# Hybrid block on one core: VectorE's splits ordered two by two behind its reads of banks in the Down stage, the forget column copied by VectorE, filler between attention's first score pieces

## The chip, the cores and the metric

The kernel runs on one core of one Trainium2 chip. The metric is the device time of one execution in microseconds. The core has five engines that work from queues of their own: TensorE (PE in the profile) multiplies matrices and writes the results into the eight banks of PSUM, VectorE (DVE) and ScalarE (ACT) read those banks and work elementwise, GpSimd (POOL) works elementwise on SBUF alone, and SyncE (SP) issues most of the DMAs. Each engine takes its instructions strictly in the order of its queue.

## The reference

One layer of a streaming encoder, on 16 meta tokens followed by 1,024 tokens of 1,024 features, all in float32:

```
h   = concat(meta, x)
xn  = rmsnorm(h)
q, k, v, f, u, gates = split(xn @ w_in)
F   = cumsum(log_sigmoid(f + b_forget))            # one column per head, 8 heads
p   = softmax(q k^T / 8 + F[t] - F[s], s <= t)
y_a = (p v) @ w_attn_out
z   = gelu(s5(u)) @ w_glu;   y_s = z_left * sigmoid(z_right)
h   = h + (sigmoid(g1) * y_a + sigmoid(g2) * y_s) @ w_o
xn  = rmsnorm(h)
a   = conv3(xn @ w_up);      h = h + (silu(a_gate) * a_val) @ w_down      # 2,816 hidden features
out = rmsnorm(h) without the meta tokens
```

## The kernel before, in words

**Precision.** A float32 operand is used as two parts of a shorter format. ScalarE copies it into the short format (the high part); the low part is the operand less its high part, a subtraction called a *split* (`split_lo`, L136, whose instruction carries line L137). Each product is then three matmuls: high by high, high by low, low by high. A split by VectorE or GpSimd has two inputs in SBUF, unless its source lies in a bank.

**Order.** A planner places each engine's instructions by a simulation of the whole program; a call `after(a, b)` (L132) adds that a stands behind b in its engine's queue, without a wait. In attention TensorE's order is written out by hand (`pin`).

**The stages**, with their places in the span: projections of u and the state-space part with the gates (to about 180 us); the projection of q and k for the first pair of heads, the forget rows and the gated product of z (to about 310 us); the values; attention (343 to 620 us); the output products (to 745 us); the feed-forward products (to 1220 us); and the Down stage (to the end).

**The forget rows** (`forget_steps`, L551). They run as a side line while `project_qk(0)` (L593) projects k. VectorE takes the absolute value, ScalarE exponential and logarithm (L555), VectorE a minimum (L558) and the cumulative sum by a scan (L559). The columns are held in two halves, one on partitions 0 to 7, the other on 32 to 39. ScalarE copies the last column of the first half, 8x1, into `ct` (L560); VectorE's L561 adds it to the second half and scales; GpSimd's queue stores both halves to `f_d` (L563). Around it ScalarE copies k out of the banks (L608, L611), and VectorE takes its low parts.

**The gated product** (`glu`, L684) follows, by `seven` (L215): a 2x2 block product in seven block products instead of eight. `weight_forms` (L258) makes seven operands out of four weight blocks: sums on GpSimd (`sf`, L699), high parts on ScalarE (`ops`, L693), low parts on VectorE or, for two of seven, on GpSimd. In `seven` the first product's bank is copied by ScalarE into `c` (L243) before the third product may go on adding into that bank; the second product's bank is added to `c` by VectorE (L240).

**Attention.** Units of work are a pair of heads, a group of two or three row tiles and a head of the pair. For each row tile `scores` (L826) issues two matmuls into a bank of the two called `sp` (L853, L854); VectorE reads it with the forget row added and a running minimum (L859), ScalarE exponentiates (L864), GpSimd scales (L866). `scores` yields after each bank. Between such pieces TensorE gets *filler*, matmuls of the next pair's projections and of the gates, by `take(n)` (L954), which takes n of them from a stream. Before the loop over units stands a lead (L1037 to L1043): 24 filler matmuls, the first tiles' scores of unit 0, 7 filler, its last tile's scores, 14 filler, the first scores of unit 1, 7 filler. What is left of pair 0's filler is spread over its units.

**The Down stage** (from L1481). The product with `w_down` is again seven block products, numbered 0 to 6, for each of four groups of two or three pairs of row blocks: `groups = [(8, 9), (7, 0, 1), (2, 3, 4), (5, 6, 10)]`, taken in the order 0, 4, 1, 2, 5, 3, 6. A product (`product`, L1628) has four tiles of 128 rows, each in a bank of its own: two sets of four banks (`mm`, `mm`, `mm`, `po` and `sp`, `tp`, `sp`, `tp`) take turns. Products 4, 5 and 6 go on adding into the banks of 0, 1 and 3 (`JOINS`), once these have been read. VectorE reads each tile's bank and adds it into the result (L1657); the instructions that do so are appended to `first_add`. Three tiles of operands make 9 matmuls per bank and 36 per product.

`forms(p, j)` (L1517) makes the operands of product p for pair j: a load of the weight sum, for most pairs an in-place sum of the activations on GpSimd (L1526 for product 1, L1528 for 2, L1530 for 3, L1532 for 6), two high parts on ScalarE (L1539) and two splits, by GpSimd for products 0, 4 and 5 and by VectorE for 1, 2, 3 and 6 (L137). `prepare` (L1689), called ahead of each `product`, issues the forms as far ahead as the 14 operand slots allow: in the middle groups, three products. The next group's activations are loaded into tiles that the last in-place use of this group sets free. Some orders are there already: splits of group 0 and the last splits of the last group are put behind certain reads by `after`.

Of the kernel before, what the change touches and what calls it, by code (L numbers as in the profile page):

```python
# [25 lines left out]
H = 8  # L26
# [32 lines left out]
def block_kernel(ctx, tc, x, meta, xbt, x0t, g1t, w_q, w_k, w_v, w_f, w_u, w_g, b_f, w_ao, lam_d, bw_d, cw_d,  # L59
# [5 lines left out]
    V, S, GP, PE, SY = nc.vector, nc.scalar, nc.gpsimd, nc.tensor, nc.sync  # L65
# [66 lines left out]
    def after(inst, first):  # L132
        tc.add_manual_dep(inst.ins, first.ins.name, mybir.DependencyInfo(
            mybir.DependencyClass.NoSync, mybir.DependencyReason.DATA), reason="order")

    def split_lo(eng, out_, src, hi):  # L136
        return eng.tensor_tensor(out_, src, hi.bitcast(F), ALU.subtract)  # L137
# [74 lines left out]
    def m_ps():  # L212
        return pp.tile([P, 512], F, tag="mm", name="mm", bufs=3)
# [193 lines left out]
    for k0, n in FIRST:  # L407
        j, sl = k0 // 2, slice(k0 % 2, k0 % 2 + n)
# [120 lines left out]
    HL = L // 2  # L529
# [21 lines left out]
    def forget_steps(fl_, fx, ct, behind):  # L551
        after(V.scalar_tensor_tensor(out=fx, in0=fl_, scalar=-1.0, in1=fl_, op0=ALU.mult, op1=ALU.max), behind)
        for k_ in (dict(func=AF.Exp, scale=-1.0), dict(func=AF.Ln, bias=one[:FR])):
            ev = yield
            act = S.activation(fx, fx, **k_)  # L555
            after(act, ev)
            yield act
        V.scalar_tensor_tensor(out=fx, in0=fl_, scalar=0.0, in1=fx, op0=ALU.min, op1=ALU.subtract)  # L558
        V.tensor_tensor_scan(fl_, one[:FR].broadcast_to([FR, HL]), fx, 0.0, ALU.mult, ALU.add)  # L559
        S.copy(ct[32:], fl_[:H, HL - 1:])  # L560
        V.tensor_scalar(fx, fl_, ct, -8.0, ALU.add, ALU.mult)  # L561
        for r, a in ((0, 0), (32, HL)):
            GP.dma_start(f_d[:, a:a + HL], fx[r:r + H])  # L563
        yield
# [255 lines left out]
    def pin(inst):  # L820
        if pinned[0] is not None:
            after(inst, pinned[0])
        pinned[0] = inst
        return inst
# [129 lines left out]
    def take(n):  # L954
        for _ in range(n):
            mm = next(stream, None)
            if mm is not None:
                pin(mm)
# [30 lines left out]
    def fill_of(pr):  # L989
        gens, cnt = [], 0  # L990
        if pr < last_pair:
            tiles_of[pr + 1] = qk_tiles(pr + 1)
            gens.append(project_qk(pr + 1, tiles_of[pr + 1]))
            cnt += QKN
        for i in range(sum(GA[:pr]), sum(GA[:pr + 1])):
            gens.append(gate_chunk(i, ap, True))
            cnt += GAN
        return chain_(*gens), cnt
# [24 lines left out]
    def scores_of(u, which):  # L1023
        if u >= len(units):
            return
        pr, cs, e = units[u]
        if which == 0 and cs[0] == 0:
            if e == 0 and pr == last_pair:
                spares.append(spare_tiles())
            fb = ap.tile([P, L], F, tag="fb", name="fb", bufs=2)  # L1030
            SY.dma_start(fb, f_d[2 * pr + e].partition_broadcast(P))
            fbs[pr, e] = fb
        done = pts_of.setdefault(u, [])
        for c in tiles_at(u, which):
            yield from scores(tiles_of[pr], e, c, fbs[pr, e], done)

    stream, cnt = fill_of(0)  # L1037
    take(24)
    cnt -= 24
    for u, which, n in ((0, 0, 7), (0, 1, 14), (1, 0, 7)):  # L1040
        for _ in scores_of(u, which):
            pass
        take(n)  # L1043
        cnt -= n
    for u, (pr, cs, e) in enumerate(units):
        if cs[0] == 0 and e == 0:
            if pr:
                stream, cnt = fill_of(pr)
# [432 lines left out]
    groups = [(8, 9), (7, 0, 1), (2, 3, 4), (5, 6, 10)]  # L1481
# [35 lines left out]
    def forms(p, j):  # L1517
        b_ = down1.tile([P, 512], F, tag="w", name="wr", bufs=8)
        behind(SY.dma_start(b_, w_block(*own_w[p], j) if p in own_w else t_d[p][P * j:P * j + P]), j)

        if j not in SUMMED:
            r = pairs[j]
            a11, a21, a12, a22 = (r[k, h_] for k in range(2) for h_ in range(2))
            sub, add = ALU.subtract, ALU.add
            if p == 1:
                GP.tensor_tensor(a11, a11, a21, sub)  # L1526
            elif p == 2:
                GP.tensor_tensor(a11, a22, a11, add)  # L1528
            elif p == 3:
                GP.tensor_tensor(a21, a22, a21, sub)  # L1530
            elif p == 6:
                GP.tensor_tensor(a11, a11, a12, sub)  # L1532
            a_ = (a11, a11, a11, a21, a12, a22, a11)[p]
        else:
            a_ = load_form(p, j)
        slot = ops.pop(0)
        eng = GP if p in (0, 4, 5) else V
        for q, src in ((0, a_), (2, b_)):
            hi = S.copy(slot[q], src)  # L1539
            if first_copy and j in groups[0] and p >= 5:  # L1540
                after(hi, first_copy[1])
            cut = split_lo(eng, slot[q + 1], src, slot[q])
            if first_add and eng is V and j in groups[0] and p > 2:
                after(cut, first_add[1 if p == 3 else 3])
            if eng is V and j in groups[-1] and p == 6:
                after(cut, first_add[-1])
        return slot

    first_add, first_copy = [], []

# [75 lines left out]
    def product(g, p, slots, first, last):  # L1628
        l_, r_ = HALF
        joins = p in JOINS  # L1630
        whole = (0, 512)
        parts = [(t, whole) for t in range(4)]
        if last and p in (3, 6):
            parts[3:] = [(3, (0, 288)), (3, (288, 224))]
            if p == 3:
                held["end"] = m_ps()
        bks = banks(g, p)
        for t, (c0, n) in parts:
            bk = held["end"] if last and p in (3, 6) and c0 else bks[t]
            top, bot = hs[t], hs[4 + t]  # L1640
            to_, o = {0: (u2[t], 0), 1: (bot, 512), 2: (u2[t], 0), 3: (bot, 512),
                      4: (top, 0), 5: (bot, 0), 6: (top, 512)}[p]
            ts_ = slice(P * t, P * t + P)
            ps = bk[:, c0:c0 + n]
            for i, (ah, al, bh, bl) in enumerate(slots):
                k_ = dict(skip_group_check=True)
                PE.matmul(ps, ah[:, ts_], bh[:, c0:c0 + n], start=(i == 0 and not joins), stop=False, **k_)  # L1647
                PE.matmul(ps, ah[:, ts_], bl[:, c0:c0 + n], start=False, stop=False, **k_)  # L1648
                PE.matmul(ps, al[:, ts_], bh[:, c0:c0 + n], start=False, stop=(i == len(slots) - 1), **k_)  # L1649
            to = to_[:, o + c0:o + c0 + n]  # L1650
            if first and p == 0:
                first_copy.append(S.copy(to, ps))
            elif first and p in (1, 5):

                S.activation(to, ps, AF.Copy, scale=-1.0 if p in MINUS else 1.0)
            else:
                first_add.append(V.tensor_tensor(to, to, ps, ALU.subtract if p in MINUS else ALU.add))  # L1657
            if g == 2 and p == 3:
                GP.dma_start(bot, h_d[P * (4 + t):P * (4 + t) + P], accum_op=ALU.add)
            if last and p == 6:  # L1660
                row_done(t, slice(512 + c0, 512 + c0 + n), first_add[-1], t == 3)
                if t == 3 and c0:
                    rows_end(t)
                continue
            if last and n == 288:
                continue
            if not last:
                continue
            if p in (2, 1, 5):
                d_, op = {2: (bot[:, l_], ALU.add), 1: (bot[:, r_], ALU.subtract), 5: (top[:, r_], ALU.subtract)}[p]  # L1670
                GP.tensor_tensor(d_, d_, u2[t], op)
            if p in (5, 3):
                after(add_square(*sums_.pop(0)), first_add[-1])
            if p == 4:
                sums_.append((t, square(t, l_)[0]))
            elif p == 5:
                sums_.append((4 + t, square(4 + t, l_)[0]))
                GP.tensor_tensor(top[:, l_], top[:, l_], gfB[:, l_], ALU.mult)
                GP.tensor_tensor(bot[:, l_], bot[:, l_], gfB[:, l_], ALU.mult)
            elif p == 3:  # L1680
                row_done(4 + t, r_, first_add[-1])
# [37 lines left out]
    for g, p in turns:  # L1719
        prepare()  # L1720
        if (g, p) == (1, 0):
            SY.dma_start(gfB, gf.partition_broadcast(P))
        product(g, p, ready[g, p], g == 0, g == len(groups) - 1)
        ops += ready[g, p]


# [402 lines left out]
```

## Time and profile before

| | |
|---|---|
| median of 3 runs | 1434.75 us (1433.96 to 1434.91) |
| the profiled execution | 1433.68 us, its span 1431.9 us |
| TensorE clock granted | 0.998 |
| DMA | 216.17 MB, 151 GB/s in the mean |

In the rows of the trace, an instruction is given with its start and duration, engine, line, operation, the tile that it writes and those it reads, its shape, and in brackets the time that its engine stood idle before it and what ended that. Matmuls of one queue overlap: the next starts before the one before has ended. The stages by the busy time of the engines, a row per stretch:

```profile
155.00:330.00 175.00, 173.31 (x1200) 164.60 (x1199) 125.28 (x214) 86.83 (x177) 87.05 (x113) 1.00 0.49 134
330.00:620.00 290.00, 287.73 (x1992) 277.37 (x1991) 179.25 (x631) 152.41 (x358) 148.66 (x287) 1.00 0.35 95
...
1220.00:1432.00 212.00, 201.70 (x902) 166.62 (x900) 165.08 (x208) 93.05 (x183) 166.61 (x122) 0.99 0.53 167
```

The columns are the stretch, its length, then the busy time and number of instructions of TensorE, of its weight loads, of VectorE, ScalarE and GpSimd, the granted clock, the busy share of the DMA engines and GB/s.

### The profile page before, as it was taken

To read this page: it belongs to the slowest core of one execution; us is meant where nothing else is said; L and a number is where in the kernel's file an instruction comes from. 1 tells how busy PE (TensorE), PEld (TensorE's weight loads), DVE (VectorE), ACT (ScalarE), POOL (GpSimd) and SP (SyncE) were. 2 spreads that over 40 slices of the span, in tenths; PEclk is the share of its full clock that TensorE was granted. 3 is DMA by queue.
4 is the path that set the end of the run, shared out by engine and by line. 5 is a ranking of instruction groups with operands and counts; after the bars stand their busy time and mean duration, and the time that the engine had idled before them with its cause. 6 is when DMAs were issued, how large, how long until landed. Compare 5 with 4: busy or idle time off the path is not lost.

```text
span 1431.9 us, 26324 instructions
## 1 busy us (share of the span) xinstructions
PE 1411.9 (99%) x9607; PEld 1335.8 (93%) x9607; DVE 1069.9 (75%) x2050; ACT 710.2 (50%) x1382; POOL 757.1 (53%) x869
## 2 busy tenths in 40 slices
PE   8999999999999999999999999999999999999997
PEld 8999999988999999999889999999999999887886
DVE  7999788843667675666479977778876776788867
ACT  7647575423555555534546444444444345643433
POOL 1542248642456547326771344645546544887795
PEclk9999999999999999999999999999999999999999
DMA  8685645530156532077953246666753327964343
GB/s 307 169 184 160 161 98 152 157 119 30 53 155 163 124 95 72 23 267 270 225 156 130 74 111 184 182 183 166 177 141 121 97 79 250 332 204 144 109 94 118
DMA packets 93318, 216.17 MB, mean 151 GB/s; under 512 B 14802, under 2 KB 22610, under 8 KB 92804
## 3 DMA queue, kind: packets, MB, share of 16 engines
q1 hardware_dynamic: 74340, 170.28, 36.4%
q0 software_dynamic: 17696, 41.29, 15.1%
q10 hardware_dynamic: 1152, 2.91, 0.6%
q8 instruction: 76, 1.25, 0.4%
q14 instruction: 54, 0.44, 0.1%
HBM read 170.88 MB, written 71.71 MB: 169 GB/s over the span
## 4 chain that ended last, share of the span: by engine, by line
PE 56%; issue 1%; DVE 0%; POOLq 0%; DVEq 0%; ACT 0%; POOL 0%; ACTq 0%
PE sp L235 4%; PE sp L234 4%; PE sp L236 4%; PE tp L235 2%; PE tp L234 2%; PE tp L236 2%; PE mm L236 2%; PE mm L234 2%; PE mm L235 2%; PE mm L1649 2%; PE mm L1648 2%; PE mm L1647 2%; PE mm L1314 2%; PE mm L1315 2%; PE mm L1313 2%; PE sp L1647 1%
## 5 line engine op out<-in xcount | busy, mean ns | idle before, releaser
L172 PE MATMUL mm<-xhi,whi 128*128 128x342 f32 (+2 forms) x480 | 156.0, 325 | 0.0
L173 PE MATMUL mm<-xlo,whi 128*128 128x342 f32 (+2 forms) x480 | 155.4, 324 | 0.0
L174 PE MATMUL mm<-xhi,wlo 128*128 128x342 f32 (+2 forms) x480 | 154.4, 322 | 0.0
L1269 POOL TENSOR_TENSOR ov<-ov,og 128x1024 f32<-128x1024 f32 x21 | 50.8, 2420 | 119.6 <-ACT og L1268 117.2
L137 DVE TENSOR_TENSOR sw<-sf,sw 128x512 fp32r<-128x512 f32 x72 | 71.7, 996 | 45.2 <-ACT sw L1260 44.2
L1260 ACT CAST sw<-sf 128x512 fp32r<-128x512 f32 x72 | 44.9, 623 | 110.5 <-POOL sf L1407 79.4
L172 PEld LDWEIGHTS mm<-xhi,whi 128*128 128x128 f32 x480 | 90.4, 188 | 1.1 <-issue 0.6
L174 PEld LDWEIGHTS mm<-xhi,wlo 128*128 128x128 f32 x480 | 90.3, 188 | 0.5
L173 PEld LDWEIGHTS mm<-xlo,whi 128*128 128x128 f32 x480 | 90.4, 188 | 0.4
L1407 POOL TENSOR_TENSOR sf<-raw,sf 128x512 f32<-128x512 f32 x36 | 62.4, 1732 | 38.8 <-DVE sw L137 38.7
L236 PE MATMUL mm<-xhi,sw 128*128 128x258 f32 (+1 forms) x288 | 81.0, 281 | 0.0
L234 PE MATMUL mm<-xhi,sw 128*128 128x258 f32 (+1 forms) x288 | 80.8, 280 | 0.0
L1407 POOL TENSOR_TENSOR sf<-raw 128x512 f32<-128x512 f32 x36 | 48.7, 1352 | 60.6 <-DVE sw L137 32.1
L235 PE MATMUL mm<-xlo,sw 128*128 128x258 f32 (+1 forms) x288 | 80.7, 280 | 0.0
L864 ACT ACTIVATE pt<-pt,mx 128x400 f32<-128x400 f32 (+5 forms) x72 | 53.1, 737 | 45.7 <-DVE mx L859 45.3
L866 POOL TENSOR_SCALAR pt<-pt,mx 128x400 f32<-128x400 f32 (+5 forms) x72 | 51.8, 720 | 33.2 <-DVE mx L865 26.3
L1459 DVE SCALAR_TENSOR_TENSOR ov<-hv,cwt,ov 128x1024 f32<-128x1024 f32 x36 | 68.1, 1892 | 0.4 <-ACT ov L1457 0.4
L1260 ACT CAST sw<-raw 128x512 fp32r<-128x512 f32 x70 | 43.1, 622 | 47.4 <-PE sp L236 25.0
L904 ACT CAST th<-tp 128x512 fp32r<-128x512 f32 (+1 forms) x80 | 43.4, 542 | 37.3 <-PE tp L901 27.9
L137 DVE TENSOR_TENSOR sw<-raw,sw 128x512 fp32r<-128x512 f32 x70 | 57.9, 831 | 4.1 <-ACT sw L1260 3.9
L137 DVE TENSOR_TENSOR tl<-tp,th 128x512 fp32r<-128x512 f32 (+1 forms) x80 | 50.7, 634 | 10.7 <-ACT th L904 10.1
L835 POOL CAST qz<-q 64x128 fp32r<-64x128 f32 (+1 forms) x72 | 20.2, 283 | 69.4 <-PE sp L854 68.1
(722 smaller groups left out, 5724.5 us busy)
## 6 DMA issues: line engine op xcount, KB each, us to landing
raw<-in_w_up_dram SPq DMA_DIRECT2D x44, 512.0 KB, 3.7
t_d<-in_w_dn_dram POOLq DMA_DIRECT2D x44, 256.0 KB, 6.8
wr<-t_d SPq DMA_DIRECT2D x44, 256.0 KB, 3.3
ar<-a_d SPq DMA_DIRECT2D x41, 256.0 KB, 4.8
a_d<-ov SPq DMA_DIRECT2D x18, 512.0 KB, 2.6
wr<-in_w_dn_dram SPq DMA_DIRECT2D x33, 256.0 KB, 3.7
t_d<-in_w_dn_dram SPq DMA_DIRECT2D x22, 256.0 KB, 4.3
t_d<-t_d SPq DMA_DIRECT2D x22, 256.0 KB, 5.4
```

The source lines that it names most:

```text
L137: return eng.tensor_tensor(out_, src, hi.bitcast(F), ALU.subtract)
L172: yield PE.matmul(ps, whi[:, i, :], ahi[:, i], start=(i == 0), stop=False)
L173: yield PE.matmul(ps, whi[:, i, :], alo[:, i], start=False, stop=False)
L174: yield PE.matmul(ps, wlo[:, i, :], ahi[:, i], start=False, stop=(i == k - 1))
L234: PE.matmul(ps, a[0][:, i], bh, start=(i == 0 and not joins), stop=False, skip_group_check=True)
L235: PE.matmul(ps, a[0][:, i], bl, start=False, stop=False, skip_group_check=True)
L236: PE.matmul(ps, a[1][:, i], bh, start=False, stop=(i == kh - 1), skip_group_check=True)
L864: S.activation(pt[:n, :kc], pt[:n, :kc], AF.Exp, bias=low, scale=-1.0, accum_out=nm[:n, 0:1])
L866: GP.tensor_scalar(pt[:n, :kc], pt[:n, :kc], nm[:n, 1:2], 1.0, ALU.mult, ALU.mult)
L1260: S.copy(hi, src)
L1407: sums.append(GP.tensor_tensor(f_, a, b, op))
L1459: V.scalar_tensor_tensor(out=o, in0=h_[:, j:SEQ + j], scalar=cwc(j, m), in1=o, op0=ALU.mult, op1=ALU.add)
```

## The change

Three edits. In the Down stage, VectorE's splits for groups 1 and 2 that were issued since the last product are collected; once the next product is issued, splits 0 and 1 are put behind its first read of a bank in VectorE's queue, 2 and 3 behind the second, and so on. The forget column is copied by VectorE instead of ScalarE. In the lead of attention the filler is taken after each score piece instead of after all of them: 4 + 4, 14, 4 + 4 matmuls instead of 7, 14, 7.

```
@@ forget_steps
         V.tensor_tensor_scan(fl_, one[:FR].broadcast_to([FR, HL]), fx, 0.0, ALU.mult, ALU.add)
-        S.copy(ct[32:], fl_[:H, HL - 1:])
+        V.tensor_copy(ct[32:], fl_[:H, HL - 1:])
@@ the lead of attention
-    for u, which, n in ((0, 0, 7), (0, 1, 14), (1, 0, 7)):
+    for u, which, n in ((0, 0, 4), (0, 1, 14), (1, 0, 4)):
         for _ in scores_of(u, which):
-            pass
-        take(n)
-        cnt -= n
+            take(n)
+            cnt -= n
@@ forms
             cut = split_lo(eng, slot[q + 1], src, slot[q])
+            if eng is V and j in (*groups[1], *groups[2]):
+                splits_.append(cut)
@@ the loop over products
+        n_add = len(first_add)
         product(g, p, ready[g, p], g == 0, g == len(groups) - 1)
+        reads = first_add[n_add:]
+        if reads:
+            for i, cut in enumerate(splits_):
+                after(cut, reads[min(i // 2, len(reads) - 1)])
+        splits_.clear()
```

More of the change, by code (lines that the diff above doesn't have):

```diff
@@ L1547, in forms @@
         return slot
-    first_add, first_copy = [], []
+    first_add, first_copy, splits_ = [], [], []
     held = {}
```

## The prediction

> **What bounds the kernel now.** I read the page first, then TensorE's waits, then the instructions in order of time around each wait.
>
> ```profile
> span 1431.9 us, 26324 instructions
> PE 1411.9 (99%) x9607; PEld 1335.8 (93%) x9607; DVE 1069.9 (75%) x2050; ACT 710.2 (50%) x1382; POOL 757.1 (53%) x869
> ```
>
> TensorE is busy for 99% of the span, and no other engine for more than 75%. Whatever takes no matmul away can therefore win only TensorE's idle time. The table of TensorE's waits names it:
>
> ```profile
> PE mm L353 <- ACT uh L411: 5.5, 1, 5.5
> PE sp L1647 <- DVE hs L1657: 1.8, 1, 1.8
> PE mm L234 <- ACT c L243: 1.7, 1, 1.7
> ```
>
> The first lies at the start of the program, which the diff doesn't touch. The second and third are single waits, and the diff has an edit at each; its third edit lies at a wait of 0.42 us (below). So there are three places, and I cost each from its own rows.
>
> **Edit 1, the Down stage.** TensorE's instructions in order of time, at its wait:
>
> ```profile
> 1297.80 0.39 PE L1649 MATMUL tp<-op 128*128 128x512 f32 x1
> 1298.02 0.39 PE L1647 MATMUL mm<-xhi 128*128 128x512 f32 x1
> 1300.18 0.50 PE L1647 MATMUL sp<-xhi 128*128 128x512 f32 x1 [1.77 <-DVE hs L1657]
> ```
>
> Matmuls overlap, so what a wait costs is start to start: 1300.18 - 1298.02 = 2.16, against 0.22 between the two starts before it: 1.94 us lost. What came here is product 6 of group 1, which adds into the banks of product 3 and must wait until VectorE has read them. VectorE at that time:
>
> ```profile
> 1290.65 5.96 DVE L137 TENSOR_TENSOR op<-ar,op 128x512 fp32r<-128x512 f32 x1
> 1296.54 0.68 DVE L137 TENSOR_TENSOR op<-wr,op 128x512 fp32r<-128x512 f32 x1
> 1297.14 1.78 DVE L137 TENSOR_TENSOR op<-ar,op 128x512 fp32r<-128x512 f32 x1
> 1298.85 0.68 DVE L137 TENSOR_TENSOR op<-wr,op 128x512 fp32r<-128x512 f32 x1
> 1299.45 0.68 DVE L1657 TENSOR_TENSOR hs<-hs,sp 128x512 f32<-128x512 f32 x1
> ```
>
> Four splits (L137) stood ahead of the read (L1657) in VectorE's queue. Product 3's first bank was full about 9 x 0.23 = 2.1 us after the product began; the read came at 1299.45. The splits took 0.68, 1.78 and once 5.96 us. POOL shows why:
>
> ```profile
> 1284.74 1.30 POOL L137 TENSOR_TENSOR xlo<-wr,xlo 128x512 fp32r<-128x512 f32 x1
> ...
> 1294.74 1.33 POOL L137 TENSOR_TENSOR op<-wr,op 128x512 fp32r<-128x512 f32 x1
> 1296.70 1.68 POOL L1528 TENSOR_TENSOR ar<-ar 128x512 f32<-128x512 f32 x1 [0.63 <-DVE op L137]
> ```
>
> POOL ran nine instructions of two SBUF inputs without a gap from 1284.74 to 1296.07, and the split ended only after that run. The last row also tells whose the four splits are: L1528 is product 2's in-place sum, and it waits for the splits of product 1 of the next group. That form is issued three products ahead, in the step of product 6 of group 1. By the new lines its splits 0 and 1 go behind the first read of that product 6, 2 and 3 behind its second, 4 and 5 behind its third. None can then stand ahead of product 3's reads, and the forms issued with product 3 itself are POOL's. So this wait should go: -1.94 us. If my assignment were wrong and the four belonged to product 3's own step, they would stand behind its first read, and the wait would go too; that the edit misses its target isn't a case.
>
> What it adds: no instruction and no wait on another engine, only an order in VectorE's queue. The 48 splits of groups 1 and 2 come up to one product (36 x 0.23 = 8.3 us) later. Queued behind them are POOL's in-place sums (L1526 to L1532), POOL's splits behind those, ScalarE's casts of the sums, and SyncE's loads of the next group into the freed tiles. A form is wanted three products after its issue, which leaves two products, some 16 us. Cover that is gone would show at the hand-overs, below.
>
> **Edit 2, the forget column.** ScalarE's queue, and TensorE's wait:
>
> ```profile
> 208.26 0.73 ACT L555 ACTIVATE fg<-fg,one 40x520 f32<-40x520 f32 x1
> 211.67 0.19 ACT L560 COPY fg<-fg 8x1 f32<-8x1 f32 x1 [2.67 <-DVE fg L559]
> 211.88 0.41 ACT L693 CAST ops<-sf 128x256 fp32r<-128x256 f32 x1
> ...
> 214.35 0.66 ACT L243 COPY c<-mm 128x260 f32<-128x260 f32 x2
> ```
>
> ```profile
> 212.69 0.28 PE L234 MATMUL tp<-z1h,ops 128*128 128x260 f32 x1
> 212.81 0.28 PE L235 MATMUL tp<-z1l,ops 128*128 128x260 f32 x1
> 214.78 0.39 PE L234 MATMUL mm<-zh,ops 128*128 128x260 f32 x1 [1.69 <-ACT c L243]
> ```
>
> ScalarE stands 2.67 us at the head of its queue with a copy of 8x1, because VectorE's scan isn't done. Two casts, two k copies, two casts and the two copies of c then follow one another, and TensorE waits for c: 214.78 - 212.81 = 1.97, less 0.12, is 1.85 us. With the copy on VectorE, ScalarE goes on at 209. What it waits for next is TensorE and POOL:
>
> ```profile
> 209.47 0.28 PE L234 MATMUL mm<-zh,ops 128*128 128x260 f32 x1
> ```
>
> ```profile
> 208.52 0.74 POOL L699 TENSOR_TENSOR sf<-raw 128x256 f32<-128x256 f32 x1
> 212.66 1.06 POOL L563 DMA_DIRECT2D f_d<-fg  x2 [3.40 <-DVE fg L561]
> 213.73 0.74 POOL L137 TENSOR_TENSOR ops<-sf,ops 128x256 fp32r<-128x256 f32 x1
> ```
>
> The sum to be cast is ready at 208.52 + 0.74 = 209.26, the k block's last matmul has started by 209.47. From 209.3 the same six instructions take 214.35 - 211.88 = 2.47 us, so c is copied from 211.8 to 212.4, and TensorE wants it at 212.81 + 0.12 = 212.93: 0.5 to spare, and the whole 1.85 us goes. Next late is the low part of the second cast's operand. POOL still issues its DMAs at 212.66, since VectorE's L561 stays where it was, and the split ends at 213.73 + 0.74 = 214.47. TensorE's next matmuls on it:
>
> ```profile
> 216.58 0.28 PE L236 MATMUL tp<-z1h,ops 128*128 128x260 f32 x1
> ```
>
> Shifted by 1.85 that is 214.73: 0.26 to spare.
>
> What it adds is a copy on VectorE, of a form that this trace doesn't show. From above it is bounded by a copy of 512 columns, from below by nothing, and what it replaces is the 0.26 us in which VectorE waited for ScalarE's:
>
> ```profile
> 342.04 0.42 DVE L782 COPY mv<-mv 16x512 f32<-16x512 f32 x1
> ```
>
> ```profile
> 211.89 0.48 DVE L561 TENSOR_SCALAR fg<-fg 40x520 f32<-40x520 f32 x1 [0.26 <-ACT fg L560]
> 213.63 1.12 DVE L137 TENSOR_TENSOR kl<-mm,k 64x384 fp32r<-64x384 f32 x2 [1.25 <-ACT k L611]
> ```
>
> So L561 moves by -0.26 to +0.16. I take 0, since ScalarE's 8x1 copy took 0.19 and is the nearest in size. Behind it VectorE had 1.25 us of waiting for the k copies that now goes. SyncE's queue gains too: its transfers of k wait for the same copies.
>
> **Edit 3, filler between the first scores.** TensorE and VectorE:
>
> ```profile
> 344.77 0.34 PE L174 MATMUL mm<-xhi,wlo 128*128 128x384 f32 x1
> 344.94 0.34 PE L172 MATMUL mm<-xhi,whi 128*128 128x384 f32 x1
> 345.70 0.40 PE L853 MATMUL sp<-k,q 128*128 128x272 f32 x1 [0.42 <-DVE mx L859]
> ```
>
> ```profile
> 345.48 0.16 DVE L859 CUSTOM_DVE_ANT_0 pt<-sp,fm 16x16 f32<-16x16 f32 x1
> ```
>
> The third score tile needs the bank of the first, read until 345.64. The wait costs 345.70 - 344.94 - 0.17 = 0.59. The edit puts 4 + 4 filler matmuls where 7 were: one more, 0.17 us, ahead of that point. If VectorE reads when it did, 0.17 is all that is won; if the new order lets the read pass the q splits queued before it, up to 0.59. I take 0.2. The two fillers more in all (30 for 28) come off pair 0's later shares and cost nothing, since TensorE does the same matmuls in the end.
>
> **The sum.** 1.94 + 1.85 + 0.2 = 4.0 us. The profiled execution took 1433.68 us, its span being 1431.9; it would come to 1429.7. It stands 1.07 below the median of the runs, 1434.75, from which the forecast is 1430.8.
>
> **Rivals.**
>
> *A new wait at a hand-over in the Down stage.* Product 3 of group 2 passes its banks at once to product 6, and there the profile is already tight:
>
> ```profile
> 1356.44 0.68 DVE L1657 TENSOR_TENSOR hs<-hs,mm 128x512 f32<-128x512 f32 x1
> ```
>
> ```profile
> 1357.65 0.39 PE L1647 MATMUL mm<-xlo 128*128 128x512 f32 x1
> ```
>
> The read ends at 1357.12, 0.5 us before TensorE wants the bank. The edit moves six splits into the 8.2 us of product 2 of group 2, where VectorE now rests between reads, four times about like this:
>
> ```profile
> 1337.22 0.69 DVE L1657 TENSOR_TENSOR u<-u,mm 128x512 f32<-128x512 f32 x1 [1.35 <-PE mm L1649]
> ```
>
> Some 5.4 us of rest (4 x 1.35) take six splits of 0.68 (4.1), but not six of 1.78 (10.7): the overflow is 0 to 5.3 us, and all over 0.5 of it reaches TensorE, if the order there stays. For it: the read in question is already queued behind splits. Against it: POOL's sums, and with them those splits, come later too and may fall behind the read. With one pair of the three slowed (6.3) the overflow is 0.9 and the wait 0.4; with two (8.5), 3.1 and 2.6. The sum is then 3.6 to 1.4: 1431.2 to 1433.4, and 1435.6 if all three are. Chance 0.25.
>
> *POOL's low part ends last in edit 2.* If the new order puts the matmuls on it ahead of those on c, TensorE waits from 212.93 to 214.47, 1.54 of the 1.85. The sum is 2.5: 1432.3. For it: POOL's 3.40 us of waiting stays. Against it: the order of before has them behind. Chance 0.12.
>
> *Slower: splits starved between reads.* In product 0 of group 2 the splits of product 2 go two by two between reads whose banks product 4 wants 6.2 us later (three tiles of 2.05). If the first split of each pair meets a POOL run as at 1290.65, a pair takes 5.96 + 0.68 = 6.6. First read done at 2.7, second at 10.1 (wanted at 10.3), third at 17.4 (wanted at 12.3), fourth at 24.7 (wanted at 14.4, or 19.5 after the wait). It decides from the second starved pair on: 5.1 us, then 10.3, against the 4.0: 1435.9 to 1441.0. For it: the 5.96. Against it: the run quoted lasts 11.3 us, no more than two pairs. Chance 0.06, two thirds of it over the bound.
>
> [...]
>
> The rest, 0.07: the planner orders something else anew, with a sum of 0 to 2.5.
>
> **How the numbers follow.** About 0.2% of the time, 2.9 us, is what a measurement of this kernel can tell from no change. The likeliest case (0.50) gives 4.0, and its own range is 3.3 to 4.8 (c or the low part late by up to 0.6; the third edit's 0.59, and the 0.1 by which the first matmul after a wait is slower, three times), of which 0.48 is over the bound. The hand-over case is over it in a third (0.08), the rest in 0.02: faster 0.58. Slower 0.05: the starved case 0.04, the rest 0.01. Same 0.37. The range goes from 1434.75 - 4.8 = 1429.9 to 1434.4, past two slowed pairs at the hand-over; some 0.15 is left out.
>
> **What would show it.** Right: TensorE's waits on L1657, on c L243 and on mx L859 near 345 are gone or down to some tenths; in product 3 of group 1 VectorE reads each bank within 0.1 us of its last matmul; ScalarE's row of L560 is gone and its casts start by 209.4. Wrong: a new wait on L1657 near 1356 or at the start of product 4 of group 2, a wait of tp in L236 on POOL's ops, or a split of over 4 us right between two reads.

## The result, and the profile after

The changed kernel takes 1439.06 us (median of 9 runs, 1436.21 to 1441.01), the kernel before 1434.75 in the same rounds: a ratio of 1.0029 with a 95% interval of 1.0018 to 1.0040, that is 2.6 to 5.7 us slower, some 0.3%. The forecast was 1430.8, range 1429.9 to 1434.4.

The profiled execution took 1439.48 us. From its page:

```profile
span 1437.7 us, 26308 instructions
PE 1416.6 (99%) x9607; PEld 1337.6 (93%) x9607; DVE 1067.9 (74%) x2051; ACT 709.3 (49%) x1381; POOL 762.6 (53%) x869
```

TensorE has the same 9607 matmuls and is busy for 4.7 us longer, its idle time grew by only 1.1. So part of the loss must be matmuls that ran slower. The table of TensorE's waits (us in total, times, longest):

```profile
PE mm L353 <- ACT uh L411: 5.1, 1, 5.1
PE mm L1648 <- DVE hs L1658: 2.7, 1, 2.7
...
PE sp L853 <- DVE mx L859: 1.1, 2, 0.8
```

The 1.8 us on `sp L1647` and the 1.7 us on c are gone, as forecast. In their place stands a single wait of 2.7 us on the same kind of read (line numbers are one higher from the Down stage on). TensorE's instructions there, in order of time:

```profile
1358.74 0.39 PE L1648 MATMUL sp<-op 128*128 128x512 f32 x1
1361.79 0.64 PE L1648 MATMUL mm<-xlo 128*128 128x512 f32 x1 [2.66 <-DVE hs L1658]
1362.23 0.63 PE L1649 MATMUL mm<-xlo 128*128 128x512 f32 x1
```

It is the passage from product 3 to product 6 of group 2, the place of the first rival. Start to start it costs 1361.79 - 1358.74 - 0.23 = 2.82 us. The matmuls behind it take 0.63 instead of 0.39 and start 0.44 apart instead of 0.23. The same stretch in windows of 1 us (the clock is the third column from the right):

```profile
1361.00:1362.00 1.00, 0.21 (x1) 0.21 (x2) 1.00 (x3) 0.00 (x0) 1.00 (x1) 0.99 0.04 12
1362.00:1363.00 1.00, 1.00 (x3) 0.80 (x3) 1.00 (x2) 0.00 (x0) 1.00 (x3) 0.50 0.60 176
1363.00:1364.00 1.00, 1.00 (x4) 0.73 (x3) 1.00 (x3) 0.00 (x0) 1.00 (x2) 0.50 0.42 102
1364.00:1365.00 1.00, 1.00 (x4) 0.81 (x3) 1.00 (x2) 0.53 (x2) 1.00 (x3) 0.50 0.77 111
1365.00:1366.00 1.00, 1.00 (x4) 0.79 (x4) 0.88 (x2) 1.00 (x3) 1.00 (x3) 0.80 1.00 193
```

The granted clock is 0.5 right behind the wait. What is missing to full speed sums to 0.01 + 3 x 0.50 + 0.20 = 1.71 us, that is 3.4 us at half the clock. Wait and clock together: 4.53 us. VectorE ahead of it:

```profile
1336.50 0.69 DVE L1658 TENSOR_TENSOR u<-u,mm 128x512 f32<-128x512 f32 x1 [1.35 <-PE mm L1650]
1337.11 0.68 DVE L137 TENSOR_TENSOR xlo<-ar,xlo 128x512 fp32r<-128x512 f32 x1
1337.71 1.77 DVE L137 TENSOR_TENSOR xlo<-wr,xlo 128x512 fp32r<-128x512 f32 x1
1339.41 0.67 DVE L1658 TENSOR_TENSOR u<-u,mm 128x512 f32<-128x512 f32 x1
...
1346.22 1.77 DVE L137 TENSOR_TENSOR op<-ar,op 128x512 fp32r<-128x512 f32 x1
1347.91 0.68 DVE L1658 TENSOR_TENSOR u<-u,po 128x512 f32<-128x512 f32 x1
...
1357.46 1.41 DVE L137 TENSOR_TENSOR xhi<-wr,xhi 128x512 fp32r<-128x512 f32 x1
1358.79 1.75 DVE L137 TENSOR_TENSOR xhi<-ar,xhi 128x512 fp32r<-128x512 f32 x1
1360.46 0.68 DVE L137 TENSOR_TENSOR xhi<-wr,xhi 128x512 fp32r<-128x512 f32 x1
1361.06 0.67 DVE L1658 TENSOR_TENSOR hs<-hs,mm 128x512 f32<-128x512 f32 x1
```

From 1337 until that wait ends VectorE never rests. Where it rested 1.35 us between two reads in the kernel before, it now works on splits, seven ahead of the fourth read, four of them at 1.77 us; that fourth read of product 2 comes at 1347.91, and the backlog lasts until the read at 1361.06, with three splits still right ahead of it, as in the kernel before.

To see where the whole 5.8 us between the two profiled spans lie, I compare the start times of matmuls with the same number: +0.7 up to 200 us, where nothing differs between the kernels; +0.2 over the gated product; -0.2 in attention's lead; +2.7 in the rest of attention and behind it; -2.1 at the wait near 1298; +4.5 at the hand-over. Sum 5.8. The +2.7 needs an explanation too.

### The profile page after: what moved, and what is told of

It is laid out like the page before. It is cut to its first block, busy times and chain, and to the rows that moved or that the text cites. A ratio compares the mean times of both kernels' runs of the same rounds, so it can differ in the third digit from the quotient of the medians.

```text
span 1437.7 us, 26308 instructions
## 1 busy us (share of the span) xinstructions
PE 1416.6 (99%) x9607; PEld 1337.6 (93%) x9607; DVE 1067.9 (74%) x2051; ACT 709.3 (49%) x1381; POOL 762.6 (53%) x869
## 4 chain that ended last, share of the span: by engine, by line
PE 54%; DVE 1%; issue 1%; DMA 1%; POOL 0%; ACT 0%; POOLq 0%; DVEq 0%; SPq 0%
PE sp L235 4%; PE sp L234 4%; PE sp L236 4%; PE tp L234 2%; PE tp L235 2%; PE tp L236 2%; PE mm L236 2%; PE mm L234 2%; PE mm L235 2%; PE mm L1648 2%; PE mm L1649 2%; PE mm L1650 2%; PE mm L1313 2%; PE mm L1314 2%; PE mm L1312 2%
```

## The experiments

Start times of same-numbered matmuls give, for every profiled execution, the length of a stretch without what happened ahead of it. Three are used below: 9000 to 9250 (from 1287 us, with the place of the wait near 1298), 9250 to 9400 (from 1346 us, with the hand-over) and 2700 to 3500 (from 395 us, attention). In the kernel before they are 59.01, 34.15 and 112.61 us.

### Each edit alone, and edit 1 in one step

`split_only`, `copy_only` and `fill_only` are edits 1, 2 and 3 of the diff, each by itself. `split_step16` is edit 1 with

```
-        if reads:
+        if reads and (g, p) == (1, 6):
```

> Edit 1 alone; the other two as before. Hand-over theory (edit 1 moves its wait to the passage from product 3 to product 6 of group 2 and makes it dearer): the wait of 1.77 us near 1298 is gone, -2.1; in its place a wait on VectorE's read near 1360 of 2.5 +/- 0.5 us, whose start-to-start cost is 2.8, and behind it about 3.4 us at a granted clock of 0.5, another 1.7; sum +2.4, median near 1437.2, slower by 0.1 to 0.25%. Rival (the loss comes from edits 2 and 3, edit 1 is worth what was forecast): no wait over 1 us near 1360, median near 1432.8.

> Edit 2 alone. Theory: the wait on c is gone (-1.9), about half of it comes back as short waits on VectorE's low parts and on the state space scan behind it, since nothing else upstream of the edit differs; -1.0 to -1.9, median 1432.9 to 1433.8, no new wait in attention. Rival (the copy of 8x1 on VectorE delays its queue, and attention pays for it): a wait on mx L859 near 443 as with all three edits, median 1434.5 to 1436.

> Edit 3 alone. Theory (edit 3 pays for its 0.2 with a new order of TensorE, VectorE and GpSimd in the first pair of heads): the wait near 346 falls from 0.42 to about 0.26, and waits on mx L859 near 443 (0.8) and on ob L944 near 453 (0.3) appear, +1.5 to +2 in all; median 1436.3 to 1436.8. Rival (those waits come from the stages ahead running 1 to 2 us earlier, not from the filler): no wait over 0.5 us between 400 and 460, median 1434.4 to 1434.7.

> Edit 1 cut down to the splits issued with product 6 of group 1, which are those of product 1 of group 2; all others stand where they stood in the kernel before. Theory: these four splits alone made the wait near 1298, and the wait near 1360 comes from the splits issued with later products being held back; so the wait near 1298 is gone, VectorE reads the last bank of product 3 of group 2 where it did before, no wait over 0.5 us near 1360 and no fall of the clock; median near 1432.7. Rival (the delay of product 1's splits alone fills VectorE in product 2 of group 2): a wait of over 1 us near 1360, median 1434.5 or more.

| kernel | median us | ratio to before, 95% | 9000-9250 | 9250-9400 |
|---|---|---|---|---|
| split_only | 1439.63 | 1.0035 (1.0022 to 1.0047) | 56.92 | 38.66 |
| copy_only | 1433.98 | 0.9996 (0.9983 to 1.0008) | 56.92 | 34.15 |
| fill_only | 1434.76 | 1.0004 (0.9990 to 1.0018) | 56.92 | 34.15 |
| split_step16 | 1434.90 | 1.0004 (0.9993 to 1.0015) | 56.92 | 34.15 |

Edit 1 alone is as slow as all three. TensorE's waits of `split_only`:

```profile
PE mm L1649 <- DVE hs L1659: 2.7, 1, 2.7
```

The hand-over theory holds, and split_step16 says that the splits issued with product 6 of group 1 have no part in it. But the second column was in no expectation: copy_only and fill_only have the Down stage of the kernel before, and both took 56.92 us, not 59.01. The wait that edit 1 was to remove isn't there in them.

Some expectations were missed. copy_only has lost its wait on c, but the median shows no gain clear of the noise. fill_only has the wait on mx that its theory named, 0.9 us near 447, but not the 1.5 to 2 us in the median; its profiled execution, 1438.09 us, lies 3.3 us above that median. split_step16 is 2 us above its forecast, since in most executions the wait that it removes isn't there.

### The wait near 1298 belongs to single executions

`before_again` is the kernel before, unchanged, profiled once more.

> The kernel before, unchanged, for a second profile of it. Theory (the wait near 1298 belongs to single executions: VectorE's first split there is sometimes starved by GpSimd for 5.96 us and mostly shares with it for 0.9): no wait over 0.5 us near 1298, and about 56.9 us instead of 59.0 from matmul 9000 to matmul 9250. Rival (this order of the queues always makes it): the wait of 1.8 us is there again.

It took 1432.26 us, and 56.92 us from matmul 9000 to 9250. VectorE, at the place of the split of 5.96 us:

```profile
1291.33 1.02 DVE L137 TENSOR_TENSOR op<-ar,op 128x512 fp32r<-128x512 f32 x1
1292.27 1.77 DVE L137 TENSOR_TENSOR op<-wr,op 128x512 fp32r<-128x512 f32 x1
1293.97 1.77 DVE L137 TENSOR_TENSOR op<-ar,op 128x512 fp32r<-128x512 f32 x1
1295.66 1.78 DVE L137 TENSOR_TENSOR op<-wr,op 128x512 fp32r<-128x512 f32 x1
1297.37 0.67 DVE L1657 TENSOR_TENSOR hs<-hs,sp 128x512 f32<-128x512 f32 x1
```

The same four splits stand ahead of the read, and POOL is as busy, but no split takes longer than 1.78 us, and POOL's instructions beside them take 1.74 or 1.75 after a first one of 1.30. The read comes 6.0 us after the first split began, in the profile of before 8.8; that is the difference between no wait and one of 1.8. Of the nine profiled executions in which the queues at this place are those of the kernel before, two have the 5.96 us and the wait: the profile that I forecast from, and `step22_last2` below:

```profile
1292.10 5.96 DVE L137 TENSOR_TENSOR op<-ar,op 128x512 fp32r<-128x512 f32 x1
1297.98 0.68 DVE L137 TENSOR_TENSOR op<-wr,op 128x512 fp32r<-128x512 f32 x1
```

So what edit 1 removes is worth about 2/9 x 2.1 = 0.5 us on average, a rough figure from nine executions.

### Which splits make the hand-over wait

`only_step22` is edit 1 with the condition `(g, p) == (2, 2)`, `all_not_step22` all three edits with `(g, p) != (2, 2)`. Step (2, 2) issues the splits of product 6; in the kernel before VectorE ran four of the six ahead of its first read of product 1 and the other two ahead of the fourth.

> Edit 1 for the splits issued with product 2 of group 2 alone (those of product 6); everything else as in the kernel before. Theory: these six, which ran ahead of VectorE's reads of product 1 in the kernel before and now stand between its reads of product 2, make the whole hand-over wait: a wait of 2.5 +/- 0.4 us near 1360 and a granted clock of 0.5 behind it, +4.5; median near 1439. Rival (the backlog comes from all the splits that were held back in groups 1 and 2 together): no wait over 1 us near 1360, median 1434 to 1435.5. Near 1298 nothing is changed against the kernel before: the wait of 1.8 us is there or not, as in other executions without edit 1 (one of three so far).

> All three edits, but the splits issued with product 2 of group 2 stay where they were. Theory: no wait near 1298, none over 0.5 us near 1360, clock 1.0 throughout; edit 2's wait gone; median 1432.5 to 1434.5, some 5 us under the changed kernel. Rival (another step's splits make the hand-over wait as well): a wait of over 1 us near 1360, median over 1436.

only_step22: 1437.08 us (some 2 us under what was expected), ratio 1.0023 (1.0011 to 1.0034), 38.65 us from matmul 9250 to 9400, and in TensorE's waits

```profile
PE mm L1649 <- DVE hs L1659: 2.6, 1, 2.6
```

all_not_step22: 1432.11 us, ratio 0.9991 (0.9981 to 1.0001), 34.73 us, clock 1.0. TensorE at the hand-over:

```profile
1354.66 0.39 PE L1648 MATMUL sp<-op 128*128 128x512 f32 x1
1355.34 0.50 PE L1648 MATMUL mm<-xlo 128*128 128x512 f32 x1 [0.30 <-DVE hs L1658]
```

Six splits out of 48 make nearly the whole wait: with the other 42 held, 0.3 us of it is left. All of the change but these six costs nothing that was measured, and may win 1 us.

Why these six are dear shows in the kernel before, where the fourth of them and GpSimd's next instruction were

```profile
1327.60 0.68 DVE L137 TENSOR_TENSOR op<-wr,op 128x512 fp32r<-128x512 f32 x1
1333.34 1.36 POOL L137 TENSOR_TENSOR op<-ar,op 128x512 fp32r<-128x512 f32 x1 [13.56 <-ACT op L1539]
```

GpSimd stood idle for 13.56 us there, and each of the six took 0.68 or 0.69 us, 4.1 in all. The edit moved them into product 2, where GpSimd works; the same six, the first of the seven splits counted above, took 0.68 + 2 x 1.18 + 2 x 1.77 + 1.78 = 8.4 us.

### Number of splits or their places, length of the wait or its place

Edit 1 for step (2, 2) alone, with other lines in place of the loop over the splits:

```
step22_last2       for cut in splits_[4:]:  after(cut, reads[2])
step22_last4       for i, cut in enumerate(splits_[2:]):  after(cut, reads[1 + i // 2])
step22_first4      for cut in splits_[:4]:  after(cut, reads[0])
step22_all_first   for cut in splits_:  after(cut, reads[0])
```

> Edit 1 for step 22 alone, and only the last two of its six splits are held, behind VectorE's third read of product 2 of group 2. Theory: two splits of about 1.8 us less ahead of the reads than with all six, 1.8 each in the worst case: a wait of 0 to 0.5 us near 1360, matmul 9250 to 9400 in 34.2 to 34.7 us, clock 1.0.

> The last four of the six are held, two behind the second and two behind the third read. Theory: between the two neighbours, a wait of 0.5 to 2 us near 1360. If the length of the wait decides on the clock, a wait under 1.8 us costs itself alone (34.2 + wait, clock 1.0 behind it), one over 2.6 costs 1.7 us more; if the place decides, half the clock follows whatever the wait.

> The first four of the six are held, all behind the first read of product 2; the last two stay free. Theory: about as with the last four, a wait of 0.5 to 2 us near 1360, and the same rule for the clock behind it.

> All six are held, all behind the first read instead of two by two. Theory (the number of splits that the product has to take in decides, not their places between its reads): the wait of 2.6 us near 1360 and the half clock behind it are there as with two by two, matmul 9250 to 9400 in 38.6 us. Rival (the two-by-two order, whose later splits stand between reads, makes it): no wait over 1 us.

| splits held | wait at the hand-over | 9250-9400 | above 34.15 |
|---|---|---|---|
| none (kernel before) | none | 34.15 | - |
| last two | 0.56 | 35.00 | 0.85 |
| last four | 1.20 | 35.63 | 1.48 |
| first four | 1.42 | 35.82 | 1.67 |
| six, two by two | 2.63 | 38.65 | 4.50 |
| six behind the first read | 2.75 | 38.75 | 4.60 |

Each of these four kernels was timed in one execution, so only the stretches are compared; the 1443.79 us of step22_all_first also hold a stop of 2.40 us near 141 and 6.8 us at half the clock behind it. The wait grows with the number of splits held, by 0.28 to 0.46 us a split held, and the two-by-two places matter little: six behind one read are no better. (With the first four the profile names ScalarE's cast of an operand as what came last; VectorE's read ended at the same time, 0.15 us before the restart.) Behind 1.20 us, in step22_last4, the clock stays up (windows of 1 us),

```profile
1358.00:1359.00 1.00, 0.62 (x3) 0.54 (x4) 1.00 (x2) 0.00 (x0) 1.00 (x2) 1.00 0.25 59
1359.00:1360.00 1.00, 1.00 (x6) 0.83 (x5) 1.00 (x3) 0.00 (x0) 1.00 (x2) 1.00 0.56 203
```

and behind 2.75 us, in step22_all_first, it is down (one window of 4 us; 4 x (1 - 0.57) = 1.7 us lost):

```profile
1366.00:1370.00 4.00, 3.88 (x10) 3.06 (x11) 3.88 (x6) 1.20 (x3) 4.00 (x5) 0.57 0.71 129
```

### Stops of another origin

Three kernels set stops into the kernel before: ahead of one tile's matmuls, in products that add into full banks, ScalarE copies the bank that TensorE wants into scratch, n times.

```
+            if t == 2 and (g, p) in IDLE:
+                S.copy(sq[:, :256], bks[1][:, :256])
+                for _ in range(IDLE[g, p]):
+                    S.copy(sq[:, :256], bk[:, :256])
```

> The kernel before with eight stops of TensorE set into the Down stage, at products that nothing else makes wait: in front of the third tile of products that add into full banks, ScalarE copies the bank before and then 3 to 9 times the bank itself, into scratch, and the matmuls must wait for it; the stops should be about 1 to 3.5 us. Theory (a stop of more than about 2.2 us is followed by half the clock for 3.4 us, a shorter one is not): granted clock 1.0 behind the stops up to 1.8 us, near 0.5 for 3.4 us behind those of 2.7 and more, each dear by another 1.7 us. Rival (the fall of the clock near 1362 has another cause, the load of the engines or the place): no fall behind a stop of 2.7 us, or falls behind 1.2 us too.

> The kernel before with two stops set into the Down stage, at product 6 of group 1 and at product 6 of group 2: ScalarE copies the bank before and then 4 times the bank that TensorE wants, into scratch. From the stop of 2.76 us that 5 such copies made, at 0.40 us a copy, each should be 2.36 us. Theory (the clock is judged over stretches of about 3.4 us by the share of idle time; 2.66 of 3.41 brought it down, 1.77 did not): a stop of 2.36 us lies between and falls or not by where it stands in its stretch; if it falls, 3.4 us at 0.5 start within 3.4 us of the restart. Rival (any stop of over 2 us brings it down): half the clock behind both. Other rival (only stops of over 2.6 us do): clock 1.0 behind both.

> The same with 6 copies at product 6 of group 1 (a stop of about 3.16 us) and 3 at product 6 of group 2 (about 1.96 us). Theory and both rivals: half the clock for 3.4 us behind the first. Behind the second: theory and the second rival say clock 1.0, the first rival, taken to 1.9 us, half.

Most stops didn't come about, since the planner put other tiles' matmuls in their place: seven of the eight in idle_ladder are 0.1 us or nothing, those of the other two kernels at most 0.33. So the planned row of lengths didn't come about, and the stops of the other two kernels tell nothing of the clock. The one that came, in idle_ladder:

```profile
1372.70 0.50 PE L1652 MATMUL mm<-xlo 128*128 128x512 f32 x1 [2.76 <-ACT sq L1649]
```

```profile
1373.00:1374.00 1.00, 1.00 (x6) 0.78 (x5) 0.00 (x0) 1.00 (x3) 0.75 (x1) 0.97 0.00 0
1374.00:1375.00 1.00, 1.00 (x4) 0.81 (x3) 0.00 (x0) 1.00 (x3) 1.00 (x2) 0.50 0.00 0
1375.00:1376.00 1.00, 1.00 (x4) 0.81 (x3) 0.01 (x1) 1.00 (x3) 1.00 (x2) 0.50 0.00 0
1376.00:1377.00 1.00, 1.00 (x4) 0.71 (x4) 0.67 (x1) 1.00 (x3) 1.00 (x2) 0.50 0.18 29
1377.00:1379.00 2.00, 2.00 (x10) 1.64 (x9) 1.20 (x2) 1.90 (x4) 2.00 (x3) 0.91 0.35 117
```

ScalarE made this stop, VectorE is idle behind it, and the price is the same: 0.03 + 1.50 + 2 x 0.09 = 1.71 us. Here the clock falls about 1.2 us after the restart, in the changed kernel 0.2 us after it. The times of the falls say why. In the changed kernel the first full clock at 10.31, the fall at 1361.99 and the one behind the last matmuls at 1433.67 lie whole multiples of 3.413 us apart, 396 and 21 times; in fill_only 9.63, 217.85 and 1432.99 do, 61 and 356 times; and so it is in all 18 traces. So the clock changes on a grid of stretches of 3.41 us that the stops don't shift. The stretch ahead of the fall held 2.66 us of idle TensorE in the changed kernel, and 2.17 of the 2.76 us in idle_ladder.

Stops that nobody set show that length alone doesn't decide. From the waits of fill_only and of step22_first4:

```profile
PE mm L234 <- ACT c L243: 1.7, 1, 1.7
PE sp L2026 <- DMA U<-u_d: 2.4, 1, 2.4
```

and the stretches of the grid behind them, one of fill_only and two of step22_first4:

```profile
217.85:221.26 3.41, 3.41 (x16) 3.41 (x17) 2.06 (x5) 1.17 (x5) 1.83 (x3) 0.50 0.90 242
141.42:144.83 3.41, 1.84 (x14) 1.70 (x15) 3.27 (x10) 1.48 (x4) 0.00 (x0) 1.00 0.13 44
144.83:148.24 3.41, 3.41 (x26) 3.11 (x26) 1.33 (x3) 1.94 (x5) 0.54 (x1) 1.00 0.00 0
```

The 1.69 us of fill_only lay whole in one stretch, 214.43 to 217.85, and half the clock followed. The 2.45 us of step22_first4 were cut by the grid at 141.42 into 1.29 and 1.16, and nothing followed. The 1.77 us of the kernel before were cut at 1299.52 into 1.11 and 0.66. Over the 18 traces, from the first full clock on, a fall followed every stretch with more than 1.8 us of idle TensorE and none with less than 1.69; of three in between (1.69, 1.69 and 1.80) it followed one. So about half a stretch of idle time, 1.69 to 1.80 of 3.41 us, is the line in these traces, near to the theory written down for stops_23. Where the grid lies differs between executions, so by these counts a stop of 2.6 us, cut by the grid like that of 2.45, needn't always pay for the clock, though the five of 2.63 to 2.76 us that were traced all did.

### The versions without the costly step

`best_with_filler` and `best_without_filler` are split_step16 with edit 2, with and without edit 3.

> Edits 2 and 3, and edit 1 for the splits issued with product 6 of group 1 alone (so VectorE's order from product 0 of group 2 on is that of the kernel before). Theory: no wait near 1298, 1355 or 1360, the wait on c gone: at or a little under the 1432.1 of the kernel with all edits but one step, 1431.5 to 1432.5, and 1.5 to 2.5 us under the kernel before. Rival (the filler's order costs 1 us in attention on average): 0.8 to 1 us slower than the one without filler beside it.

> The same without edit 3. Theory (edit 3 gives 0.2 us in the lead of attention and the waits near 443 come from the landing of ob's store, whatever the filler): 1431.7 to 1432.7, 0.2 us above the one with filler, which these rounds cannot tell from none. Rival: 1430.7 to 1431.5, 0.8 to 1 us faster than the one with filler.

They took 1432.33 us, ratio 0.9989 (0.9978 to 1.0000), and 1431.75 us, ratio 0.9994 (0.9982 to 1.0006). No wait is left in either near 1298 or at the hand-over. Whether the filler costs 1 us these rounds don't tell: the medians lean one way, the ratios the other. Both lie well under the changed kernel, and all_not_step22 with them; against the kernel before, whose median was 1432.9 to 1433.8 in those rounds, the 0.6 to 1.7 us are at the edge of what was measured.

## Why the prediction was wrong

**The term of 1.94 us for edit 1 was a reading of one execution.** The mechanism was right: four splits of product 1 of the next group ahead of the read, issued in step (1, 6), gone by the edit (56.9 us in every kernel with it). But the price came from a split of 5.96 us that two executions of nine have. The prediction had the evidence that this duration was odd: the other splits in its rows took 0.68 and 1.78 us, and it had seen that GpSimd ran nine instructions without a gap beside this one. It used that only for the slower rival. Right size: about 0.5.

**The step that failed is the choice between a delay that two products, "some 16 us", would absorb, and the first rival.** The rival had the place, the read that is late and, with two slowed pairs, even the wait: 2.6 forecast, 2.66 measured. It got 0.25 because GpSimd's sums, and the splits that wait for them, might fall behind the read. They didn't: VectorE's order at the hand-over stayed, and everything in it came later. The rival's sum held as well: 5.4 us of rest against six splits, which took 8.4 us where its case of two slowed pairs has 8.5. What the prediction didn't weigh is that the six came from a place where GpSimd rested to one where it works; of the seven splits ahead of the fourth read of product 2, four took 1.77 us, two 1.18 and one 0.68. The 1.77 is common there while GpSimd works too, and the profile of before had it at 1342.68, some 14 us ahead of the hand-over.

**No term had the price of a stop beyond its length.** The rival's 2.6 us was entered as 2.6. It cost 4.53: 2.82 start to start, and 1.71 for the half clock, put at nothing in the prediction. Together with the mis-sized 1.94, this turns the rival from a smaller gain into a loss.

**Edit 2** did what was forecast, step by step: ScalarE's copy is gone, its casts wait for TensorE, and c is copied in time.

```profile
211.05 0.41 ACT L693 CAST ops<-sf 128x256 fp32r<-128x256 f32 x1 [0.43 <-PE mm L173]
...
213.52 0.66 ACT L243 COPY c<-mm 128x260 f32<-128x260 f32 x2
```

VectorE's copy, the operation that the trace of before didn't show, took 0.14 us:

```profile
213.35 0.14 DVE L560 COPY fg<-fg 8x1 f32<-8x1 f32 x1
```

The size was off: without the edit this wait lies between 0.6 and 1.7 us in 13 profiled executions, and I had one at the upper end. Over the stretch from matmul 1400 to 1800 the median is 52.4 us in those 13 and 51.3 in the five with the edit: 1.1 us, not 1.85. In the changed kernel's own profile nothing of it is seen (53.0 us), since VectorE came 1.7 us late into the stretch, from work upstream of the edit; fill_only, without edit 2, lost still more there (55.5), 1.7 of it by the half clock from 217.85 on.

**Edit 3** gave 0.2 in the lead, as taken: 61.18 us instead of 61.41 from matmul 2300 to 2700 in every execution with it. TensorE still waits there:

```profile
346.61 0.40 PE L853 MATMUL sp<-k,q 128*128 128x272 f32 x1 [0.26 <-DVE mx L859]
```

**The 2.7 us later in attention** seem mostly no part of the change. TensorE's new wait on mx near 443 goes back to ScalarE, which stood before its copy into `ob`, a single buffer, until the store of its last content had landed. In the changed kernel:

```profile
442.86 0.37 ACT L943 COPY ob<-po 64x256 f32<-64x256 f32 x1 [1.76 <-DMA o_d<-ob]
```

In split_only, where attention is that of the kernel before, it stood there too (the profile names TensorE, which had long been done):

```profile
441.03 0.37 ACT L943 COPY ob<-po 64x256 f32<-64x256 f32 x1 [1.37 <-PE sp L854]
```

Over the executions this wait varies from 0.08 to 1.84 us, and the stretch from matmul 2700 to 3500 with it: 112.5 to 112.6 us at 0.1, 113.3 to 113.4 at 0.5 to 0.9, 113.9 to 114.3 at 1.4 to 1.6, without the filler. The four with the filler are 113.29 at 0.4, 113.91 at 1.0 and 114.94 and 114.78 at 1.8, some 0.4 us above that line. So the filler's order may give back what it wins in the lead; four executions don't settle it.

Put together from these stretches: +4.5 - 0.5 for edit 1, -1.1 for edit 2, about 0 for edit 3, in all +2.9, at the lower end of the measured 2.6 to 5.7; between the medians, 4.3 us, some 1.4 are not accounted for.

The third rival, splits starved between reads, did not happen: in product 2 of group 2 no split took more than 1.8 us, and product 0 made no wait.

## What to carry to other kernels

A wait that one profile shows is a sample. Before an edit is priced by it, look for what makes it: if it hangs on a duration that stands apart, as that of a split of 5.96 us among splits of 1.77, profile the kernel a few times and price it by its average. When work is put behind something in the queue of an engine, look whether the rival engine rests where the work stood and works where it goes, count it at the duration that it has while that engine works (here 8.4 us for the six splits), not at its best (4.1), follow the backlog to the next place where a bank or a buffer is handed over at once, and order only the part that the wait needs: here 6 of the 48 splits made the change slower. A stop of TensorE can cost more than its length: here it did where about half of a stretch of 3.41 us on the clock's grid was idle (1.69 us in fill_only, 2.66 in the changed kernel).

## What the runs showed of the hardware

- **Stops of TensorE and its clock.** In each of the 18 traces all changes of the granted clock lay on a grid of 3.413 us. Half the clock in the middle of a kernel lasted 3.41 us, once 6.83 (step22_all_first); 3.41 us of it cost 1.7 us. What told the falls apart was TensorE's idle time within one stretch of the grid: over 1.8 us always brought the clock down, under 1.69 never. So five stops of 2.63 to 2.76 us, one of 2.40 and one of 1.69 did, and one of 2.45 and two of 1.77, cut by the grid, did not. About half a stretch was enough: 1.69 of 3.41 us in fill_only, 2.17 in idle_ladder; once 1.69 and once 1.80 were not.
- **VectorE and GpSimd on two-input work.** In the Down stage of the kernel before, VectorE's 23 splits that had no two-input instruction of GpSimd beside them took 0.68 to 0.69 us. Of the 57 that had one, 13 took 0.68 to 0.69 as well, 22 took 1.77 to 1.81, two 4.63 and 5.96, and the others lay between 0.81 and 1.62. GpSimd's sum took 1.29 us without a split beside it (at 1339.65) and 1.74 beside splits of 1.77 (at 1345.56). Longer splits are not rare elsewhere: near 725 one took 4.97 to 5.55 us in all 18 traces (why isn't shown). Nor is it shown why the split near 1291 took 5.96 us in two executions of nine (in the profile of before beside GpSimd's instructions of 1.31 to 1.33) and 1.02 in before_again.
- **The spread of this kernel** from run to run, some 7 us, is made up of single waits in part: the landing of one store of 136 KB, whose wait goes from 0.08 to 1.84 us, moved attention by 1.8 us in kernels with the same order there, a split of 5.96 us the Down stage by 2.1, and a stop of 1.69 us in fill_only cost 1.7 us more by where the clock's grid lay.
